# Hybrid decoder layer on Trainium2: in the MLP's fast products, two of seven right sides go through DRAM whole, two sums of weights come first, and the residual is scaled in wider pieces

## The chip, the cores and the metric

The kernel runs on one core of a Trainium2 chip (the chip has eight). The metric is device time in microseconds of one execution of the whole layer. It is compared as a median over several executions; a profiled execution gives the views that are read here. A core has five engines with a queue each: PE (TensorE, matrix products), DVE (VectorE), ACT (ScalarE), POOL (GpSimd) and SP (SyncE, which here issues every DMA). Each engine takes its instructions in the order in which they were put into its queue; one that waits holds up all behind it.

## The reference

One decoder layer over 1024 tokens of width 1024, in float32: two mixers side by side, cross-attention into 256 memory tokens, and a squared-ReLU MLP with a hidden width of 4096. The change lies in the MLP:

```python
D_MODEL = 1024
SEQ = 1024
D_FF = 4 * D_MODEL
...
def rmsnorm(x, g):
    xf = x.astype(jnp.float32)
    y = xf * lax.rsqrt(jnp.mean(xf * xf, axis=-1, keepdims=True) + EPS)
    return (y * g.astype(jnp.float32)).astype(x.dtype)
...
        u = jax.nn.relu(rmsnorm(x, ln2[l]) @ w_ff1[l])
        x = x + (u * u) @ w_ff2[l]
    return rmsnorm(x, ln_f)
```

## The kernel before

Activations lie with features in the partitions (128) and tokens in the free dimension, so a projection takes weights as the stationary side ("left") and activations as the moving side ("right"). A float32 operand is *split* in two parts, a high part `hi` (an ACT copy into the type that PE multiplies) and a low part `lo` = operand minus `hi` (a DVE subtraction): that is `split` (L129 to L136). A product of two split operands is three matmuls into one PSUM bank, lo·hi, hi·lo and hi·hi: `mm3` (L182 to L186).

**Seven products for eight.** Both MLP projections use the Winograd form of Strassen's scheme on 2 by 2 blocks: seven block products in place of eight, of which four take sums of left blocks and four sums of right blocks. The products are numbered 1 to 7; 1, 2 and 4 take plain blocks of the left side, 5, 6, 7 and 3 take sums. The right sides are called "11", "21", "22" and t1 to t4.

**Up projection** (L1169 to L1457). The 4096 hidden rows are cut into 16 *pairs* `p_` of two 128-row tiles, two pairs to each of 8 blocks `b`. `left_up` (L1185) loads two weight tiles r1 = (x11, x12) and r2 = (x21, x22), each 128x1024 (the pair's rooms are `wr` for an odd pair, `z` for an even one), and makes left sides in three groups: group 0 splits r1 as it is (products 1 and 2) and x22 alone into `h22`, `l22` (product 4); then four sums are formed in place, on POOL for pairs 2 to 15 and on DVE for pairs 0 and 1; group 1 splits r2, now two sums (products 5 and 6), and group 2 splits r1, now the other two (products 7 and 3). `jobs` (L1211 to L1215) is the order of the products, a job being 12 matmuls; `prepare` (L1225) cuts left sides five jobs ahead. `Pair.run` (L1326) multiplies, and puts the results together on DVE (`add`, L1324) and ACT (L1313, L1314 for the squared ReLU, L1337 for a copy `p1` of product 1).

**Between the projections** the four blocks u11, u12, u21, u22 of a pair and the sums t1 to t4 are written to DRAM (`right[b]`, a slot for each of the seven right sides with places [0] for hi and [1] for lo). `put` (L1360) splits one 128x512 tile with a hi room that `rotate("d", "e")` takes from two rooms `r_d` and two `r_e`, and stores both parts (L1364, L1365). `put_right` (L1367) lists seven steps for a pair, one step before each job. The last of the eight blocks goes to `plain` in the same way.

**The residual.** While the up projection runs, `stretch` (L1420) takes the residual `x2d` back from DRAM in 16 pieces of 128x512, multiplies each by `row` (L1428, DVE) and stores it again. A piece is loaded into an `r_d` or `r_e` room at one job and scaled two jobs later.

**Down projection** (L1459 to L1517). 28 steps `(b, m)`, seven blocks `b` by four output tiles `m`. `left` (L1398) loads one 128x1024 tile of `w_ff2q` into `wr` (two rooms), forms four sums on POOL (L1408), and splits the plain blocks into two `w4` rooms and the sums into `wh`, `wl`. `rights` (L1461) loads two right sides, hi and lo, into one `act` room; there are seven such rooms, two for the residual and four for the right sides in use, so the first pair of right sides of the next block (products 1 and 5: "11" and t1) finds a free room early. A step multiplies 7 x 2 x 3 = 42 matmuls and adds each product into the residual on DVE (L1515).

The rooms named `w4` (five of 128x1024) are shared by u22 with t1, by t2 with t4 and by the plain left sides of the down projection. The instruction order on each engine follows a list scheduler's simulated times, priorities in the order of the program text.

Of the kernel before, what the change touches and what calls it, by code (L numbers as in the profile page):

```python
# [9 lines left out]
F32 = mybir.dt.float32  # L10
F32R = mybir.dt.float32r
AF = mybir.ActivationFunctionType
ALU = mybir.AluOpType
# [6 lines left out]
TH = 512  # L20
D = 1024
KT = D // P
# [22 lines left out]
def hybrid_layer(ctx: ExitStack, tc: tile.TileContext, a: dict, out: bass.AP):  # L45
    nc = tc.nc
    v, s, g = nc.vector, nc.scalar, nc.gpsimd
# [24 lines left out]
    def w4(shape=(P, 1024), dt=F32):  # L72
        t = sb("w4", [P, 1024], 5, dt)[: shape[0]]
        return t.rearrange("p (a b) -> p a b", b=shape[2]) if len(shape) == 3 else t
# [36 lines left out]
    load = nc.sync.dma_start  # L111
# [17 lines left out]
    def split(hi, lo, src, scale=None):  # L129

        if scale is None:
            s.activation(hi, src, AF.Copy)  # L132
            return v.tensor_tensor(out=lo, in0=src, in1=hi.bitcast(F32), op=ALU.subtract)  # L133
        else:
            s.activation(hi, src, AF.Copy, scale=scale)
            return v.scalar_tensor_tensor(out=lo, in0=src, scalar=scale, in1=hi.bitcast(F32), op0=ALU.mult, op1=ALU.subtract)  # L136
# [24 lines left out]
    def rotate(*tags):  # L161

        spare[tags] = spare.get(tags, -1) + 1
        return w2(tags[spare[tags] % len(tags)])
# [23 lines left out]
    def both(pair, f):  # L188
        return f(pair[0]), f(pair[1])
# [63 lines left out]
    row = const("row", [P, T])  # L253
# [12 lines left out]
    at = 0  # L266
# [33 lines left out]
    h = [(act(), act()), (act(), act())]  # L300
# [20 lines left out]
    for k in range(KT):  # L321
        if k == 2:
            load(wg_raw, a["w_gate"])
        if k % 2 == 0:
            c = slice(k % 4 * 256, k % 4 * 256 + 512)
# [719 lines left out]
    n = 0  # L1045
# [119 lines left out]
    def sub(out_, x, y, by=v):  # L1165
        by.tensor_tensor(out=out_, in0=x, in1=y, op=ALU.subtract)
# [18 lines left out]
    def left_up(p_, group):  # L1185

        if group == 0:
            raws[p_] = raw_pair(p_, *todo[p_][2:])
        r1, r2 = raws[p_]
        x11, x12, x21, x22 = r1[:, :TH], r1[:, TH:], r2[:, :TH], r2[:, TH:]  # L1190
        hi, lo = (sb(t, [P, 1024], 3, F32R) for t in ("wh", "wl"))
        split(hi, lo, (r1, r2, r1)[group])
        if group == 0:
            h22, l22 = (w2(t, dt=F32R) for t in ("bc" if p_ else "ay"))
            split(h22, l22, x22)
            cuts[p_, 4] = both((h22, l22), lambda t: t.rearrange("p (k c) -> p k c", k=4))
            by = g if p_ > 1 else v
            sub(x11, x11, x21, by)
            by.tensor_tensor(out=x21, in0=x21, in1=x22, op=ALU.add)
            sub(x22, x22, x11, by)  # L1200
            sub(x12, x12, x22, by)
        for e in range(2):
            cuts[p_, ((1, 2), (5, 6), (7, 3))[group][e]] = both((hi, lo), lambda t: t[:, e * TH : e * TH + TH].rearrange("p (k c) -> p k c", k=4))
        if group == 2:
            del raws[p_]
# [154 lines left out]
    def put(dst, x):  # L1360

        hi = rotate("d", "e").bitcast(F32R)
        split(hi, x.bitcast(F32R), x)
        load(dst[0], hi.bitcast(F32))  # L1364
        load(dst[1], x)  # L1365

    def put_right(b, k, pair):  # L1367

        u11, u12, u21, u22 = (pair.u[c] for c in ("11", "12", "21", "22"))
        t1 = pair.t1  # L1370
        to = lambda c: [right[b][ORDER.index(c), :, p_, k] for p_ in range(2)]
        t = {}

        def one():
            sub(t1, u12, u11)
            put(to("11"), u11)

        def two():
            x = w4()
            t[2], t[4] = x[:, :TH], x[:, TH:]  # L1380
            sub(t[2], u22, t1)
            sub(u12, u22, u12, g)
            put(to("t1"), t1)

        def four():
            sub(t[4], t[2], u21)
            put(to("22"), u22)

        return [one, two, lambda: put(to("t3"), u12), four, lambda: put(to("21"), u21), lambda: put(to("t2"), t[2]), lambda: put(to("t4"), t[4])]
# [8 lines left out]
    def left(src):  # L1398

        q = sb("wr", [P, 1024], 2)  # L1400
        after[0] = load(q, src)
        q = q.rearrange("p (q c) -> p q c", q=4)
        q21, q11, q12, q22 = (q[:, i] for i in range(4))
        sums = z4()[:, :1024].rearrange("p (q c) -> p q c", q=4)
        s1, s2, s3, s4 = (sums[:, i] for i in range(4))

        for o, x, y, op in ((s1, q21, q22, ALU.add), (s2, s1, q11, ALU.subtract), (s3, q11, q21, ALU.subtract), (s4, s2, q12, ALU.subtract)):
            g.tensor_tensor(out=o, in0=x, in1=y, op=op)  # L1408
        hq, lq = (w4(dt=F32R)[:, :768].rearrange("p (q c) -> p q c", q=3) for _ in range(2))
        split(hq, lq, q[:, 1:])  # L1410
        hs, ls = (sb(t, [P, 1024], 3, F32R).rearrange("p (q c) -> p q c", q=4) for t in ("wh", "wl"))
        split(hs, ls, sums)
        f = lambda hi, lo, i: both((hi, lo), lambda t: t[:, i].rearrange("p (k c) -> p k c", k=2))
        return {1: f(hq, lq, 0), 2: f(hq, lq, 1), 3: f(hs, ls, 3), 4: f(hq, lq, 2), 5: f(hs, ls, 0), 6: f(hs, ls, 1), 7: f(hs, ls, 2)}

    stretches = [(n, hf) for n in range(KT) for hf in range(2)]

    held = []

    def stretch(n, hf):  # L1420

        x = x2d[:, n // 2, n % 2, hf]
        if not held:
            held.append(rotate("d", "e"))
            load(held[0], x)
        else:
            t = held.pop()
            v.tensor_tensor(out=t, in0=t, in1=row[:, hf * TH : hf * TH + TH], op=ALU.mult)  # L1428
            load(x, t)

    pairs = {}
# [1 line left out]
    for at, (p_, i) in enumerate(jobs):  # L1433
        prepare(at)
        for _ in range(2 if at < 2 else 1):
            if rest and at:
                rest.pop(0)()
        if at == 6:
            norm_factors(1)
        if at == 30:  # L1440
            to_row(row, inv, 8, rowd[3:4], bank)
        if at > 30 and at % 2 == 0 and stretches:
            stretch(*stretches[0])
            if at % 4 == 2:
                stretches.pop(0)
        if at == len(jobs) - 3:
            lefts = left(a["w_ff2q"][0, 0])
        if later:
            later.pop(0)()
        pair = pairs.setdefault(p_, Pair(p_))  # L1450
        pair.run(i, cuts.pop((p_, i)))
        if i == 4:
            b, k = todo[p_][:2]
            later += put_right(b, k, pair) if b < NB - 1 else put_plain(k, pair)
            del pairs[p_]
# [5 lines left out]
    def rights(b, at):  # L1461

        t = act()
        n = min(2, 7 - at)
        for e in range(n):
            load(t[:, 4 * e : 4 * e + 4].bitcast(F32), right[b][at + e].rearrange("p e k c -> p (e k) c"))
        return {SEVEN[at + e]: (t[:, 4 * e : 4 * e + 2], t[:, 4 * e + 2 : 4 * e + 4]) for e in range(n)}

    x2 = []

# [3 lines left out]
        load(x2[m // 2][:, m % 2], x2d[:, m])  # L1474

    steps = [(b, m) for b in range(NB - 1) for m in range(4)]
    r = {}
    r.update(rights(0, 0))
    r.update(rights(0, 2))
    x2_load(0)  # L1480
    r.update(rights(0, 4))
# [2 lines left out]
    def distances(op, m):  # L1484

        x = x2[m // 2][:, m % 2]
        for i, hf in ((0, 1), (1, 0)):
            g.tensor_tensor(out=x[:, i, hf], in0=x[:, i, hf], in1=x[:, 1, 1], op=op)

    for at, (b, m) in enumerate(steps):  # L1490
        now = lefts
        if m == 0:
            r_now, r = r, {}
        if at + 1 < len(steps):
            b1, m1 = steps[at + 1]
            lefts = left(a["w_ff2q"][b1, m1])
        with tc.issue_after(after[0].ins):
            if at < 3:
                x2_load(at + 1)
            if b + 1 < NB - 1:  # L1500
                for i in ((), (), (0,), (2, 4, 6))[m]:
                    r.update(rights(b + 1, i))
        if b == 0:
            distances(ALU.subtract, m)
        x = x2[m // 2][:, m % 2]
        x11, x12, x21, x22 = (x[:, i, j] for i in range(2) for j in range(2))
        held = {}

        for i, of, y, op in ((1, 1, x22, ALU.add), (5, 5, x22, ALU.add), (7, 7, x22, ALU.add), (6, 6, x22, ALU.add), (2, 1, x11, ALU.add), (4, 5, x21, ALU.subtract), (3, 7, x12, ALU.subtract)):
            if of == i:  # L1510
                held[of] = bank()
            ps = held[of]
            for k in range(2):
                mm3(ps, both(now[i], lambda t: t[:, k]), both(r_now[i], lambda t: t[:, k]), of == i and k == 0, k == 1, True)
            v.tensor_tensor(out=y, in0=y, in1=ps, op=op)  # L1515
        if b == NB - 2:
            distances(ALU.add, m)  # L1517


    us = []  # L1520
# [107 lines left out]
```

## Time and profile before

| what | value |
|---|---|
| median of three executions (lowest, highest) | 1550.0 us (1548.9, 1554.5) |
| profiled execution | 1552.39 us |
| its span, first to last instruction | 1550.6 us |
| mean granted TensorE clock | 0.995 |
| busy share PE, DVE, ACT, POOL | 97%, 71%, 47%, 29% |
| moved by DMA | 311.94 MB, mean 201 GB/s |

The page of the profile is read by part: busy times by engine, the span in 40 slices, the DMA queues, the chain of work that ended last, the costliest groups of instructions. Beside it stand views of the trace: the timeline of one engine (start, duration, engine, line, operation, output and inputs; in square brackets how long the engine was idle just before, and what ended that), a table of windows (busy time and count by engine in a stretch of time), instruction groups (count, busy time, mean duration) and the waits. Names of tiles stand without their buffer numbers.

### The profile page before, as it was taken

To read this page: it belongs to the slowest core of one execution; us is meant where nothing else is said; L and a number is where in the kernel's file an instruction comes from. 1 tells how busy PE (TensorE), PEld (TensorE's weight loads), DVE (VectorE), ACT (ScalarE), POOL (GpSimd) and SP (SyncE) were. 2 spreads that over 40 slices of the span, in tenths; PEclk is the share of its full clock that TensorE was granted. 3 is DMA by queue.
4 is the path that set the end of the run, shared out by engine and by line. 5 is a ranking of instruction groups with operands and counts; after the bars stand their busy time and mean duration, and the time that the engine had idled before them with its cause. 6 is when DMAs were issued, how large, how long until landed. Compare 5 with 4: busy or idle time off the path is not lost.

```text
span 1550.6 us, 22020 instructions
## 1 busy us (share of the span) xinstructions
PE 1511.7 (97%) x7729; PEld 1260.3 (81%) x7729; DVE 1104.4 (71%) x1742; ACT 722.3 (47%) x1351; POOL 445.1 (29%) x501
## 2 busy tenths in 40 slices
PE   8999999999999999999999999899999999999997
PEld 8878888889898887788888788677778778888887
DVE  7756676665788874844457988788877767766666
ACT  7324343334688773634444556566665422111224
POOL 0002130413455441511110023333333543333320
PEclk9999999999999999999999999999999999999999
DMA  6422323446887949953344458778777976666623
GB/s 216 126 78 82 95 104 114 130 129 164 254 257 220 314 150 304 326 166 118 116 156 146 153 168 283 253 262 288 274 249 277 382 278 243 239 243 240 244 93 110
DMA packets 124412, 311.94 MB, mean 201 GB/s; under 512 B 13822, under 2 KB 28472, under 8 KB 116364
## 3 DMA queue, kind: packets, MB, share of 16 engines
q1 hardware_dynamic: 124300, 310.52, 58.7%
q8 instruction: 61, 1.00, 0.3%
q14 instruction: 51, 0.42, 0.1%
HBM read 206.42 MB, written 104.05 MB: 200 GB/s over the span
## 4 chain that ended last, share of the span: by engine, by line
PE 76%; DVE 9%; DMA 7%; ACT 4%; issue 3%; SPq 0%; POOL 0%; DVEq 0%; POOLq 0%; ACTq 0%
PE tp L184 7%; PE tp L186 7%; PE tp L185 7%; PE mm L184 5%; PE m L184 5%; PE m L186 5%; PE mm L186 5%; PE mm L185 5%; PE m L185 5%; PE sc L184 4%; PE sc L186 4%; PE sc L185 4%; PE ov L779 2%; PE tp L760 2%; PE ov L184 2%
## 5 line engine op out<-in xcount | busy, mean ns | idle before, releaser
L184 PE MATMUL tp<-act,wl 128*128 128x512 f32 (+1 forms) x448 | 176.1, 393 | 3.4 <-DVE wl L133 2.7
L185 PE MATMUL tp<-act,wh 128*128 128x512 f32 (+1 forms) x448 | 175.4, 392 | 0.0
L186 PE MATMUL tp<-act,wh 128*128 128x512 f32 (+1 forms) x448 | 174.9, 392 | 0.0
L132 ACT ACTIVATE wh<-wr 128x1024 fp32r<-128x1024 f32 (+2 forms) x99 | 99.0, 1000 | 90.0 <-PE tp L186 33.2
L133 DVE TENSOR_TENSOR wl<-wr,wh 128x1024 fp32r<-128x1024 f32 (+2 forms) x99 | 120.4, 1216 | 26.5 <-ACT wh L132 26.2
L184 PE MATMUL mm<-act,wl 128*128 128x512 f32 (+1 forms) x336 | 130.4, 388 | 2.4 <-DVE r_e L1071 1.4
L186 PE MATMUL mm<-act,wh 128*128 128x512 f32 (+1 forms) x336 | 129.0, 384 | 0.0
L185 PE MATMUL mm<-act,wh 128*128 128x512 f32 (+1 forms) x336 | 128.7, 383 | 0.0
L184 PE MATMUL m<-act,wl 128*128 128x512 f32 (+1 forms) x312 | 120.4, 386 | 0.9 <-DVE r_a L916 0.9
L186 PE MATMUL m<-act,wh 128*128 128x512 f32 (+1 forms) x312 | 119.3, 382 | 0.0
L185 PE MATMUL m<-act,wh 128*128 128x512 f32 (+1 forms) x312 | 119.1, 382 | 0.0
L184 PE MATMUL sc<-act,wl 128*128 128x512 f32 (+1 forms) x252 | 99.5, 395 | 9.5 <-DVE wl L133 4.9
L184 PEld LDWEIGHTS tp<-act,wl 128*128 128x128 f32 x448 | 84.1, 188 | 24.2 <-DVE wl L133 4.0
L186 PEld LDWEIGHTS tp<-act,wh 128*128 128x128 f32 x448 | 84.2, 188 | 19.3
L185 PEld LDWEIGHTS tp<-act,wh 128*128 128x128 f32 x448 | 84.1, 188 | 18.8
L185 PE MATMUL sc<-act,wh 128*128 128x512 f32 (+1 forms) x252 | 98.6, 391 | 0.0
L132 ACT ACTIVATE w<-wr 128x768 fp32r<-128x768 f32 (+2 forms) x31 | 25.5, 825 | 156.6 <-PE tp L186 86.4
L186 PE MATMUL sc<-act,wh 128*128 128x512 f32 (+1 forms) x252 | 98.4, 391 | 0.0
L1408 POOL TENSOR_TENSOR z<-wr 128x256 f32<-128x256 f32 x56 | 49.7, 908 | 165.3 <-DMA wr<-w_ff2q 137.7
L132 ACT ACTIVATE wh<-z 128x1024 fp32r<-128x1024 f32 (+1 forms) x54 | 55.5, 1027 | 60.2 <-PE sc L186 25.3
L184 PEld LDWEIGHTS mm<-act,wl 128*128 128x128 f32 x336 | 63.3, 188 | 15.7 <-DVE r_e L1071 1.8
L186 PEld LDWEIGHTS mm<-act,wh 128*128 128x128 f32 x336 | 63.1, 188 | 12.8
(671 smaller groups left out, 4220.8 us busy)
## 6 DMA issues: line engine op xcount, KB each, us to landing
act<-right SPq DMA_DIRECT2D x49, 1024.0 KB
right<-w SPq DMA_DIRECT2D x56, 256.0 KB
wr<-w_ff2q SPq DMA_DIRECT2D x28, 512.0 KB
right<-r_d SPq DMA_DIRECT2D x49, 256.0 KB
right<-r_e SPq DMA_DIRECT2D x49, 256.0 KB
act<-fqk SPq DMA_DIRECT2D x48, 256.0 KB
wr<-w_in SPq DMA_DIRECT2D x20, 512.0 KB
wr<-w_ff SPq DMA_DIRECT2D x20, 512.0 KB
```

What stands on the lines that cost most here:

```text
L132: s.activation(hi, src, AF.Copy)
L133: return v.tensor_tensor(out=lo, in0=src, in1=hi.bitcast(F32), op=ALU.subtract)
L184: nc.tensor.matmul(ps, w[1], x[0], start=first, stop=False, skip_group_check=more)
L185: nc.tensor.matmul(ps, w[0], x[1], start=False, stop=False, skip_group_check=more)
L186: nc.tensor.matmul(ps, w[0], x[0], start=False, stop=last, skip_group_check=more)
L760: nc.tensor.transpose(self.ps[:, d * P : (d + 1) * P], self.pts[d][:, self.j * P : (self.j + 1) * P], ident)
L779: nc.tensor.matmul(self.ov[:, c0:], self.fv[:, self.j], t[:, c0:], start=self.j == 0 and t is self.p[1], stop=self.last and t is self.p[0])
L1408: g.tensor_tensor(out=o, in0=x, in1=y, op=op)
```

## The change

In `left_up` the two sums for products 5 and 6 are formed first, from x11, x21 and x22; then come x12 and x11, the latter from the split parts of x22 (`h22`, `l22`), so that five instructions stand where there were four. In `put_right` the right sides "11" and t1 are stored whole, once, in place of a split and two stores. `rights` loads these two (half the bytes) into the lo half of their room, and `split_whole` splits them there: for block 0 after the first loads, for the others at the end of the step that issued the load. `stretch` works on 128x1024 in a `w4` room, 8 pieces, loaded at one job and scaled four jobs later. The left side of the down projection's second step is asked for before the first right sides.

```diff
--- before.py
+++ after.py
@@ -1194,11 +1194,13 @@
             h22, l22 = (w2(t, dt=F32R) for t in ("bc" if p_ else "ay"))
             split(h22, l22, x22)
             cuts[p_, 4] = both((h22, l22), lambda t: t.rearrange("p (k c) -> p k c", k=4))
+
             by = g if p_ > 1 else v
-            sub(x11, x11, x21, by)
             by.tensor_tensor(out=x21, in0=x21, in1=x22, op=ALU.add)
-            sub(x22, x22, x11, by)
+            sub(x22, x21, x11, by)
             sub(x12, x12, x22, by)
+            sub(x11, h22.bitcast(F32), x22, by)
+            by.tensor_tensor(out=x11, in0=x11, in1=l22.bitcast(F32), op=ALU.add)
         for e in range(2):
             cuts[p_, ((1, 2), (5, 6), (7, 3))[group][e]] = both((hi, lo), lambda t: t[:, e * TH : e * TH + TH].rearrange("p (k c) -> p k c", k=4))
         if group == 2:
@@ -1373,14 +1375,14 @@
 
         def one():
             sub(t1, u12, u11)
-            put(to("11"), u11)
+            load(to("11")[1], u11)
 
         def two():
             x = w4()
             t[2], t[4] = x[:, :TH], x[:, TH:]
             sub(t[2], u22, t1)
             sub(u12, u22, u12, g)
-            put(to("t1"), t1)
+            load(to("t1")[1], t1)
 
         def four():
             sub(t[4], t[2], u21)
@@ -1413,19 +1415,19 @@
         f = lambda hi, lo, i: both((hi, lo), lambda t: t[:, i].rearrange("p (k c) -> p k c", k=2))
         return {1: f(hq, lq, 0), 2: f(hq, lq, 1), 3: f(hs, ls, 3), 4: f(hq, lq, 2), 5: f(hs, ls, 0), 6: f(hs, ls, 1), 7: f(hs, ls, 2)}
 
-    stretches = [(n, hf) for n in range(KT) for hf in range(2)]
+    stretches = list(range(KT))
 
     held = []
 
-    def stretch(n, hf):
-
-        x = x2d[:, n // 2, n % 2, hf]
+    def stretch(n):
+
+        x = x2d[:, n // 2, n % 2].rearrange("p h c -> p (h c)")
         if not held:
-            held.append(rotate("d", "e"))
+            held.append(w4())
             load(held[0], x)
         else:
             t = held.pop()
-            v.tensor_tensor(out=t, in0=t, in1=row[:, hf * TH : hf * TH + TH], op=ALU.mult)
+            v.tensor_tensor(out=t, in0=t, in1=row, op=ALU.mult)
             load(x, t)
 
     pairs = {}
@@ -1439,9 +1441,9 @@
             norm_factors(1)
         if at == 30:
             to_row(row, inv, 8, rowd[3:4], bank)
-        if at > 30 and at % 2 == 0 and stretches:
-            stretch(*stretches[0])
-            if at % 4 == 2:
+        if at > 30 and at % 4 == 0 and stretches:
+            stretch(stretches[0])
+            if at % 8 == 4:
                 stretches.pop(0)
         if at == len(jobs) - 3:
             lefts = left(a["w_ff2q"][0, 0])
@@ -1463,8 +1465,19 @@
         t = act()
         n = min(2, 7 - at)
         for e in range(n):
-            load(t[:, 4 * e : 4 * e + 4].bitcast(F32), right[b][at + e].rearrange("p e k c -> p (e k) c"))
+            if at:
+                load(t[:, 4 * e : 4 * e + 4].bitcast(F32), right[b][at + e].rearrange("p e k c -> p (e k) c"))
+            else:
+                load(t[:, 4 * e + 2 : 4 * e + 4].bitcast(F32), right[b][e][:, 1])
+                whole.append((t[:, 4 * e : 4 * e + 2], t[:, 4 * e + 2 : 4 * e + 4]))
         return {SEVEN[at + e]: (t[:, 4 * e : 4 * e + 2], t[:, 4 * e + 2 : 4 * e + 4]) for e in range(n)}
+
+    whole = []
+
+    def split_whole():
+        while whole:
+            hi, lo = whole.pop(0)
+            split(hi, lo, lo.bitcast(F32))
 
     x2 = []
 
@@ -1474,8 +1487,10 @@
         load(x2[m // 2][:, m % 2], x2d[:, m])
 
     steps = [(b, m) for b in range(NB - 1) for m in range(4)]
+    second = left(a["w_ff2q"][steps[1]])
     r = {}
     r.update(rights(0, 0))
+    split_whole()
     r.update(rights(0, 2))
     x2_load(0)
     r.update(rights(0, 4))
@@ -1493,7 +1508,7 @@
             r_now, r = r, {}
         if at + 1 < len(steps):
             b1, m1 = steps[at + 1]
-            lefts = left(a["w_ff2q"][b1, m1])
+            lefts = left(a["w_ff2q"][b1, m1]) if at else second
         with tc.issue_after(after[0].ins):
             if at < 3:
                 x2_load(at + 1)
@@ -1515,6 +1530,7 @@
             v.tensor_tensor(out=y, in0=y, in1=ps, op=op)
         if b == NB - 2:
             distances(ALU.add, m)
+        split_whole()
 
 
     us = []
```

## The prediction

> **What bounds the kernel now.** I read the busy times first, then the windows of the MLP, then PE's timeline for every idle time in it, then the timelines of the other engines just ahead of these.
>
> ```profile
> PE 1511.7 (97%) x7729; PEld 1260.3 (81%) x7729; DVE 1104.4 (71%) x1742; ACT 722.3 (47%) x1351; POOL 445.1 (29%) x501
> ```
> ```profile
> core 0: us, PE busy (x) PEld busy (x) DVE busy (x) ACT busy (x) POOL busy (x), PEclk, DMA share, GB/s
> 884.00:1216.00 332.00, 320.28 (x1361) 254.69 (x1360) 270.57 (x326) 204.21 (x320) 119.74 (x82) 0.99 0.74 259
> 1216.00:1253.00 37.00, 37.00 (x159) 29.39 (x158) 29.90 (x41) 11.36 (x15) 19.22 (x20) 1.00 1.01 385
> 1253.00:1262.00 9.00, 7.08 (x24) 5.33 (x23) 5.31 (x7) 0.85 (x1) 2.10 (x4) 0.81 1.02 419
> 1262.00:1494.00 232.00, 232.00 (x996) 185.92 (x995) 160.60 (x212) 44.36 (x47) 84.39 (x94) 1.00 0.59 226
> ```
>
> PE bounds it. The last row is PE at its pace: 232 us for 996 matmuls, 0.233 us each, no gap. So a job of 12 matmuls takes 2.8 us and a step of 42 takes 9.8 us. The change removes no matmul; all it can win is time in which PE stands still or runs slowly in the MLP. These are all of PE's waits from 884 us to 1494 us that the timeline marks, but for one of 0.7 us at 889:
>
> ```profile
> 977.03 0.50 PE L184 MATMUL sc<-act,wl 128*128 128x512 f32 x1 [0.75 <-DVE wl L133]
> 987.26 0.80 PE L184 MATMUL sc<-act,wl 128*128 128x512 f32 x1 [4.37 <-ACT r_p L1337]
> 988.28 0.63 PE L186 MATMUL sc<-act,wh 128*128 128x512 f32 x1
> 988.71 0.63 PE L184 MATMUL sc<-act,wl 128*128 128x512 f32 x1
> ...
> 1028.74 0.50 PE L184 MATMUL tp<-act,wl 128*128 128x512 f32 x1 [0.75 <-DVE wl L133]
> 1063.11 0.50 PE L184 MATMUL ov<-act,wl 128*128 128x512 f32 x1 [0.20 <-DVE wl L133]
> 1069.58 0.50 PE L184 MATMUL ov<-act,wl 128*128 128x512 f32 x1 [0.48 <-ACT r_p L1337]
> 1111.21 0.50 PE L184 MATMUL sc<-act,wl 128*128 128x512 f32 x1 [2.17 <-DVE wl L133]
> 1111.55 0.40 PE L185 MATMUL sc<-act,wh 128*128 128x512 f32 x1
> 1147.35 0.50 PE L184 MATMUL sc<-act,wl 128*128 128x512 f32 x1 [1.95 <-DVE wl L133]
> 1153.42 0.50 PE L184 MATMUL sc<-act,wl 128*128 128x512 f32 x1 [0.21 <-ACT r_p L1337]
> 1255.29 0.50 PE L184 MATMUL tp<-act,wl 128*128 128x512 f32 x1 [1.92 <-DVE wl L133]
> ```
>
> Eight gaps in the up projection sum to 10.9 us. Each restart costs 0.1 more (1111.21 to 1111.55 is 0.34, not 0.233), 0.8 in all. After the long one the matmuls start 0.43 us apart instead of 0.233 (988.28 to 988.71), for some six: 1.2. Together 12.9. In the down projection there is one gap, 1.92; in the window that holds it 24 matmuls took 7.08 us where 24 x 0.233 is 5.6, so about 1.5 went to the clock (0.81): 3.5 with the gap. **At most 16.4 us can be won.**
>
> **Where these gaps come from.** Two chains make them. The first is the four sums on POOL, here ahead of 1111.21:
>
> ```profile
> 1101.18 0.68 DVE L133 TENSOR_TENSOR r_c<-wr,r_b 128x512 fp32r<-128x512 f32 x1
> 1101.78 1.22 DVE L133 TENSOR_TENSOR wl<-wr,wh 128x1024 fp32r<-128x1024 f32 x1
> ...
> 1104.96 1.67 DVE L133 TENSOR_TENSOR w<-w,r_e 128x512 fp32r<-128x512 f32 x1
> ...
> 1109.95 1.21 DVE L133 TENSOR_TENSOR wl<-wr,wh 128x1024 fp32r<-128x1024 f32 x1
> ```
> ```profile
> 1103.08 1.30 POOL L1166 TENSOR_TENSOR wr<-wr,wr 128x512 f32<-128x512 f32 x1 [7.80 <-DVE wl L133]
> 1104.45 1.62 POOL L1199 TENSOR_TENSOR wr<-wr 128x512 f32<-128x512 f32 x1
> 1106.15 3.32 POOL L1166 TENSOR_TENSOR wr<-wr,wr 128x512 f32<-128x512 f32 x2
> ```
> ```profile
> 1107.81 1.06 ACT L132 ACTIVATE wh<-wr 128x1024 fp32r<-128x1024 f32 x1 [2.22 <-POOL wr L1166]
> ```
>
> POOL's first sum overwrites x11, so it waits for the split of r1 (1101.78, ends 1103.0). The split of r2 needs the third sum, so ACT copies its high part only at 1107.81, DVE the low part at 1109.95, and PE starts at 1111.21. DVE's own work is stretched meanwhile (1.67 for what takes 0.68 alone). The second chain is a hi room that a store has not yet given back:
>
> ```profile
> 973.09 0.63 ACT L132 ACTIVATE r_d<-w 128x512 fp32r<-128x512 f32 x1 [5.01 <-DMA x2d<-r_d]
> ```
> ```profile
> 1142.22 0.63 ACT L132 ACTIVATE r_d<-w 128x512 fp32r<-128x512 f32 x1 [4.55 <-DMA right<-w]
> ```
>
> ACT stands for 5.0 and 4.6 us, and the split of the next left side is queued behind: PE's gaps of 0.75 at 977.03 and of 1.95 at 1147.35.
>
> **The change part by part.**
>
> ```profile
> L133 DVE TENSOR_TENSOR w<-w,r_e 128x512 fp32r<-128x512 f32 x29 | 25.8, 901 | 0.2
> ...
> L133 DVE TENSOR_TENSOR wl<-z,wh 128x1024 fp32r<-128x1024 f32 x23 | 29.1, 1267 | 8.1 <-ACT wh L132 8.1
> ...
> L1428 DVE TENSOR_TENSOR r_d<-r_d,row 128x512 f32<-128x512 f32 x8 | 8.6, 1081 | 6.5 <-DMA r_d<-x2d 6.5
> ```
> ```profile
> L1166 POOL TENSOR_TENSOR z<-z,z 128x512 f32<-128x512 f32 x21 | 32.1, 1529 | 136.4 <-DVE wl L133 127.7 <-DVE r_c L133 7.9
> ```
>
> *Whole right sides.* 14 pairs x 2 = 28 splits and 28 stores of 256 KB leave the up projection: on DVE 28 x 0.90 = 25 us, on ACT 28 x 0.63 (973.09 above) = 18 us, on SP's queue 28 issues. None of this stands in a gap by itself; its worth is the rooms. Before, each pair took 7 hi rooms for puts and about 1.75 for the residual out of four, one every 2.2 us, so a room came round after 9 us; now 5, so every 3.9 us and round after 15.7 us, against a hold of some 6 us (ACT copy, DVE subtraction, a store of 4 to 5 us as the waits show). The two gaps of the second chain should close: **2.7**.
>
> The splits return in the down projection as 14 of 128x1024: 14 x 1.27 = 18 us on DVE, about as much as 14 copies of 1.06, 15 us, on ACT. There DVE is busy 160.6 of 232 us and ACT 44.4, so this lies under PE: 0, and if the cover is gone, the rival on late splits below. Seven loads of 2 MB become 1 MB; two of these (blocks 0 and 1), with the last 1 MB of removed stores, lie at 1180 to 1260 us, where DMA is full (1.01). That is 3 MB or 8 us of DMA at 385 GB/s, just ahead of the gap at 1255, which ends on weights that came late:
>
> ```profile
> 1244.92 1.43 POOL L1408 TENSOR_TENSOR z<-wr 128x256 f32<-128x256 f32 x2 [6.10 <-DMA wr<-w_ff2q]
> ```
>
> The bounds are 0 and 3.5; I take the middle, **1.8**, since the new splits come into the same engines there.
>
> *Two sums first.* x21 + x22 waits for the loads alone, and x22 new only for the split of x22 (1101.18, ends 1101.9), not for r1's. So POOL's path to the split of r2 loses r1's split (1.2), one sum (1.6), and often the first sum too: 3 to 4 us earlier. That is more than the 2.17 at 1111 and the 0.75 at 1028, which has the same shape: **2.9**. The long gap at 987 ends on ACT's copy of product 1, queued behind a square that waited for a DVE slowed by the same four sums; between 0 and 5.6 (clock included) I take two thirds, **3.7**, since the burst is cut in 2 and 3 and less DVE work meets it. Of the three small gaps (0.89) I take half, **0.45**, and of the restarts **0.6**.
>
> The price is a fifth instruction. On POOL 14 x 1.53 = 21 us, which POOL has (119.7 of 332 busy). DVE pays by being stretched: against 0.68, its two-input rows in the up projection carry some 43 us of stretch (the first row above has 29 x 0.22 = 6.4 of it) for 70 POOL operations, 0.6 each, so 14 x 0.6 = 8.6, against 25 + 7 saved. On DVE, for pairs 0 and 1, 2 x 0.69; this falls where DVE has no slack:
>
> ```profile
> 880.00:890.00 10.00, 9.27 (x41) 7.15 (x40) 10.00 (x17) 6.77 (x12) 0.00 (x0) 1.00 0.11 33
> ```
>
> Between 0 and 1.4 I take **-0.7**.
>
> *Wider residual.* The eight pieces in `r_d` rooms took 8.6 us of DVE and, taking the eight in `r_e` rooms for the same, all 17.2; 8 x 1.27 = 10.2 come in their place, and the waits for loads (6.5 in the row) should go, as the scaling now comes four jobs (11.2 us) after the load. Same bytes, 16 issues fewer on SP. Nothing beyond the rooms already counted. *Second left side asked for earlier:* its weights still need a `wr` room of the last pair; 0, between -0.5 and 0.5.
>
> **Sum:** 2.7 + 1.8 + 2.9 + 3.7 + 0.45 + 0.6 - 0.7 = 11.4. The profiled execution took 1552.4 (span 1550.6 and 1.8 around it), so 1541.0; it stood 2.4 above the median, so on the median's basis 1538.6.
>
> **The rivals.** *POOL holds DVE.* Five sums in place of four keep DVE stretched where it is 81% busy (270.6 of 332), and the gaps behind POOL stay: 987, 1028, 1111, the small ones and the restarts. For it: 1104.96 above, 1.67 for 0.68. Against: DVE loses 32 us of other work. Only the rooms and half of 1255 are won, 4.5 - 0.7: 1546. The Trainium skill, SBUF — State Buffer, "Who interferes with whom", says that a DVE instruction with two SBUF inputs and a GpSimd one that reads SBUF exclude each other for the whole of the first to start. By that a new sum can hold DVE for its full length and not for the 0.6 us that I take. The row agrees: the stretched instruction ends about when a POOL one does. With 14 x 1.53 = 21 us of stretch in place of 8.6 the saving on DVE would still be 10 us, so by this rule too the sum keeps its sign.
>
> *Late splits of the whole sides* (slower). DVE and ACT keep their order, and a split of a right side whose load has not landed holds DVE's adds, then PE's banks; or it is done too late for products 1 and 5, the first of a block. A late left side at 1255 cost 3.5 us. At all six block changes after the first that is 21 us: 1538.6 + 21 = 1560. It decides from the point at which the low part ends after the last product of the block before. Against it: two loads of the next but one block go out at 1252.59, a whole block (39 us) ahead, and DVE idles 31% of this time.
>
> ```profile
> 1252.59 1.09 SPq L1466 DMA_DIRECT2D act<-right  x2
> ```
>
> *`w4` rooms in place of hi rooms* (slower). Five rooms serve u22 with t1 (held some 10 jobs and a store of 1.6 jobs, every 7 jobs), t2 with t4 (5 and 1.6, every 7), and now the residual (4 and 1.6, every 8): 1.7 + 0.9 + 0.7 = 3.3 rooms on average. If DVE or SP waits for a store of 4.6 us at each of eight pieces, half of it reaching PE, 18 us: 1557. *The order does not come out as written:* if the scheduler leaves the sums behind other POOL work, only rooms are won: 1547.
>
> **How the numbers follow.** Gaps mostly closed 0.58, at 1538.6, its own range 1534 (all 16.4 won) to 1543. POOL holds DVE 0.18. Order lost 0.05. Late splits 0.13, `w4` rooms 0.06. What a measurement of this kernel can tell from no change is about 0.5%, 7.75 us: faster is below 1542.2. The forecast case lies there but for 0.03, so faster 0.55; same 0.03 + 0.18 + 0.05 = 0.26; slower 0.19. The range 1533 to 1555 leaves out the two slower cases, 0.19.
>
> **What would show it.** Right: no ACT wait on a store of a hi room over 1 us; POOL's first two sums ahead of r1's low part, ACT's `wh` for r2 without a wait on POOL; PE idle in the up projection below 4 us; DVE near 75% there. Wrong: a PE gap at each block change of the down projection, behind a `split` of an `act` room; DVE adds waiting for a store of `w`; PE gaps behind DVE subtractions of 1.6 us and more; DVE full and PE idle near 885 us.

## The result, and the profile after

| | before | after |
|---|---|---|
| median (lowest, highest) of 20 runs each | 1551.94 us (1548.90, 1555.96) | 1550.16 us (1545.51, 1553.21) |
| ratio, 95% interval | | 0.998 [0.9972, 0.9989] |
| span of the profiled execution | 1550.6 us | 1547.3 us |

The change wins about 2 us (3.3 us between the two profiled spans) where 11.4 were forecast. The time lies in the forecast range, the gain does not come near the forecast. First the busy times of after, then its windows over the stretches that were shown of before (columns: time, then busy time and count of PE, PEld (its weight loads), DVE, ACT and POOL, the granted clock, the DMA share, GB/s):

```profile
PE 1510.3 (98%) x7729; PEld 1261.5 (82%) x7729; DVE 1100.9 (71%) x1722; ACT 718.8 (46%) x1337; POOL 483.4 (31%) x515
```
```profile
884.00:1216.00 332.00, 320.77 (x1365) 255.96 (x1364) 256.76 (x295) 188.79 (x294) 150.47 (x96) 0.99 0.67 233
...
1253.00:1262.00 9.00, 9.00 (x41) 7.23 (x40) 5.64 (x9) 1.91 (x2) 5.57 (x8) 1.00 0.84 338
1262.00:1494.00 232.00, 232.00 (x996) 186.94 (x995) 172.74 (x222) 53.77 (x56) 88.08 (x89) 1.00 0.53 204
```

The down projection did what was hoped: 1253 to 1262 us now has PE busy throughout at full clock (before 7.08 us of 9 at 0.81), and the last row is still without a gap although the splits of the right sides are now made there (DVE 172.7 us busy, before 160.6). The up projection lost 13.8 us of DVE work, 15.4 of ACT work and 0.07 of the DMA share, and PE gained 0.5 us from it: 320.8 of 332, before 320.3. PE's timeline in the up projection (start, duration, instruction; in brackets how long PE was idle just before, and what ended that) says why:

```profile
1000.65 0.50 PE L184 MATMUL tp<-act,wl 128*128 128x512 f32 x1 [3.37 <-DVE r_f L1326]
1021.50 0.50 PE L184 MATMUL mm<-act,wl 128*128 128x512 f32 x1 [0.99 <-DVE wl L133]
1063.30 0.50 PE L184 MATMUL sc<-act,wl 128*128 128x512 f32 x1 [2.34 <-DVE r_f L1326]
1126.25 0.50 PE L184 MATMUL ov<-act,wl 128*128 128x512 f32 x1 [2.18 <-DVE r_f L1326]
1147.52 0.50 PE L184 MATMUL sc<-act,wl 128*128 128x512 f32 x1 [1.42 <-DVE wl L133]
1210.07 0.50 PE L184 MATMUL tp<-act,r_c 128*128 128x512 f32 x1 [0.19 <-DVE w L1326]
```

The gaps of before are gone but for one near 1147, which now has another cause, and others stand in their place: 10.5 us, before 10.9. The three largest (7.9 us) end on a row of a kind that no gap of before ended on, `r_f` at L1326: the DVE addition that takes a product out of its PSUM bank. PE cannot start the next product in that bank before it. DVE's timeline ahead of the gap at 1063.30, and SP's issue of the load that its first row waits for:

```profile
1056.90 1.23 DVE L1430 TENSOR_TENSOR w<-w,row 128x1024 f32<-128x1024 f32 x1 [2.22 <-DMA w<-x2d]
1058.04 0.68 DVE L1326 TENSOR_TENSOR r_p<-sc,r_p 128x512 f32<-128x512 f32 x1
1058.64 0.69 DVE L133 TENSOR_TENSOR r_c<-wr,r_b 128x512 fp32r<-128x512 f32 x1
1060.09 1.16 DVE L1166 TENSOR_TENSOR w<-w,r_p 128x512 f32<-128x512 f32 x1 [0.76 <-ACT r_p L1316]
1061.35 0.69 DVE L133 TENSOR_TENSOR r_p<-r_p,r_e 128x512 fp32r<-128x512 f32 x1
1061.96 0.69 DVE L133 TENSOR_TENSOR w<-w,r_d 128x512 fp32r<-128x512 f32 x1
1062.56 0.68 DVE L1326 TENSOR_TENSOR r_f<-sc,r_p 128x512 f32<-128x512 f32 x1
```
```profile
1051.46 0.42 SPq L1427 DMA_DIRECT2D w<-x2d  x1
```

The first DVE row is the residual's multiplication. It stands 2.22 us for its load, which was issued at 1051.46 behind a weight load and had landed 5.4 us later. Behind it in DVE's queue are two PSUM additions; the second ends at 1063.24 and PE starts at 1063.30. The wait stands six instructions ahead of the row that ends the gap. Ahead of 1000.65 and 1126.25 stand the same rows in the same order (multiplications at 994.26 and 1119.84, waits of 1.55 and 2.28). The gaps at 1021.50 and 1147.52 end on a low part `wl` that stands third behind a multiplication (1017.49 and 1143.90, waits of 1.87 and 1.59), its `wh` done before. So a waiting multiplication stands close ahead of all five gaps of more than 0.2 us, on DVE. The reverse does not hold: three of the eight waits, the longest of 4.29 us among them, made no gap. There the `r_f` addition starts 3.5 us behind the multiplication, where it takes 5.7 us ahead of the three largest gaps:

```profile
1035.74 1.23 DVE L1430 TENSOR_TENSOR w<-w,row 128x1024 f32<-128x1024 f32 x1 [2.69 <-DMA w<-x2d]
...
1039.22 0.68 DVE L1326 TENSOR_TENSOR r_f<-sc,r_p 128x512 f32<-128x512 f32 x1
```

From DVE's groups between 905 and 1216 us (count, busy, mean ns, idle before):

```profile
L133 DVE TENSOR_TENSOR wl<-z,wh 128x1024 fp32r<-128x1024 f32 x23 | 35.5, 1542 | 7.6 <-ACT wh L132 7.6
...
L1430 DVE TENSOR_TENSOR w<-w,row 128x1024 f32<-128x1024 f32 x8 | 10.2, 1275 | 19.0 <-DMA w<-x2d 19.0
```

All eight pieces waited, 19.0 us in sum. Before, five of the sixteen pieces waited, 6.5 us in the row the prediction shows and 2.2 in that of the `r_e` rooms. The text of the program puts four jobs between load and multiplication; the trace has 4.9 to 7.1 us from issue to start. The first row shows the second suspect: with five sums on POOL a low part of 128x1024 takes 1.54 us on average, before 1.27.

### The profile page after: what moved, and what is told of

It is laid out like the page before. It is cut to its first block, busy times and chain, and to the rows that moved or that the text cites. A ratio compares the mean times of both kernels' runs of the same rounds, so it can differ in the third digit from the quotient of the medians.

```text
span 1547.3 us, 21934 instructions
## 1 busy us (share of the span) xinstructions
PE 1510.3 (98%) x7729; PEld 1261.5 (82%) x7729; DVE 1100.9 (71%) x1722; ACT 718.8 (46%) x1337; POOL 483.4 (31%) x515
## 4 chain that ended last, share of the span: by engine, by line
PE 82%; DMA 7%; DVE 6%; issue 2%; ACT 2%; POOL 0%; SPq 0%; DVEq 0%; POOLq 0%; ACTq 0%
PE tp L184 7%; PE tp L186 7%; PE tp L185 7%; PE mm L184 5%; PE sc L184 5%; PE sc L186 5%; PE sc L185 5%; PE mm L186 5%; PE mm L185 5%; PE m L184 5%; PE m L186 5%; PE m L185 5%; PE ov L184 2%; PE ov L185 2%; PE ov L186 2%
## 5 line engine op out<-in xcount | busy, mean ns | idle before, releaser
L133 DVE TENSOR_TENSOR wl<-wr,wh 128x1024 fp32r<-128x1024 f32 (+2 forms) x99 | 126.3, 1276 | 26.7 <-ACT wh L132 26.3
L1410 POOL TENSOR_TENSOR z<-wr 128x256 f32<-128x256 f32 x56 | 53.5, 976 | 150.4 <-DMA wr<-w_ff2q 127.9
L133 DVE TENSOR_TENSOR wl<-z,wh 128x1024 fp32r<-128x1024 f32 (+1 forms) x54 | 73.1, 1353 | 12.4 <-ACT wh L132 12.3
```

## The experiments

Two theories stood against each other, called W and P in the expectations. **W**: the multiplication waits for its load ahead of PSUM additions. **P**: POOL's five sums stretch DVE's splits, so that these come late (the rival *POOL holds DVE*). The instruction order of each variant is made anew by the scheduler, so an edit also moves instructions that it does not name; ratios are to the kernel before, measured beside it on the same chip, with 95% intervals.

| kernel | median us | ratio |
|---|---|---|
| after, multiplication late | 1538.50 | 0.9909 [0.9897, 0.9922] |
| the same once more, other chip | 1541.72 | 0.9924 [0.9905, 0.9943] |
| after, first half of the multiplications late | 1543.59 | 0.9941 [0.9923, 0.9960] |
| after, four sums as before | 1549.29 | 0.998 [0.9968, 0.9992] |
| after, multiplication late, four sums | 1541.70 | 0.9923 [0.9910, 0.9937] |
| after, residual in halves as before | 1552.34 | 1.000 [0.9991, 1.0009] |
| before, wide residual alone | 1548.88 | 0.998 [0.9970, 0.9990] |
| before, wide residual and multiplication late | 1551.78 | 0.999 [0.9982, 0.9999] |
| before, multiplication late alone | 1560.35 | 1.0054 [1.0041, 1.0068] |
| before, five sums alone | 1557.14 | 1.0022 [1.0012, 1.0031] |
| after, multiplication late, no early second left side | 1541.82 | 0.9926 [0.9909, 0.9944] |
| after, multiplication late, sums in another order | 1534.10 | 0.9878 [0.9859, 0.9898] |

**The multiplication late.** It is put into DVE's queue behind the last PSUM addition that the program has issued by then; the load stays where it was. Taken in order, the pieces are now multiplied 15.7 to 35.4 us behind the issue of their loads, 23.6 on average where after has 5.8, so the edit moves them by more than a few instructions.

```diff
@@ Pair.run, add
-            v.tensor_tensor(out=out_, in0=ps, in1=x, op=ALU.add)
+            last_add[0] = v.tensor_tensor(out=out_, in0=ps, in1=x, op=ALU.add)
@@ stretch
-            v.tensor_tensor(out=t, in0=t, in1=row, op=ALU.mult)
+            with tc.issue_after(last_add[0].ins):
+                v.tensor_tensor(out=t, in0=t, in1=row, op=ALU.mult)
```

> The changed kernel, with the multiplication of a residual piece put behind the last PSUM add that precedes it in the program. Theory W (DVE stands at the multiplication for a load in flight, and PSUM adds queued behind it come late): DVE's wait for x2d falls from 19.0 us to under 3, PE's gaps of 3.37, 2.34 and 2.18 us and the 1.5 us of slow clock go, 8 to 9 us: ratio to before about 0.993. Theory P (the fifth sum on POOL stretches DVE, that makes the gaps): DVE's subtractions stay stretched, wl at 1.5 us, the time stays at the changed kernel's 0.998.

The median is 1538.5 us. DVE's groups, DVE's timeline at the place that made the gap of 2.34 us in after, and all of PE's gaps in the up projection:

```profile
L133 DVE TENSOR_TENSOR wl<-z,wh 128x1024 fp32r<-128x1024 f32 x24 | 39.6, 1650 | 5.3 <-ACT wh L132 5.3
...
L1433 DVE TENSOR_TENSOR w<-w,row 128x1024 f32<-128x1024 f32 x8 | 11.6, 1456 | 0.0
```
```profile
1051.03 0.68 DVE L1328 TENSOR_TENSOR r_p<-sc,r_p 128x512 f32<-128x512 f32 x1
...
1055.55 0.68 DVE L1328 TENSOR_TENSOR r_f<-sc,r_p 128x512 f32<-128x512 f32 x1
1056.15 1.22 DVE L1433 TENSOR_TENSOR w<-w,row 128x1024 f32<-128x1024 f32 x1
```
```profile
1016.18 0.50 PE L184 MATMUL mm<-act,wl 128*128 128x512 f32 x1 [0.84 <-DVE wl L133]
1056.29 0.50 PE L184 MATMUL sc<-act,wl 128*128 128x512 f32 x1 [0.64 <-DVE r_f L1328]
1076.40 0.50 PE L184 MATMUL tp<-act,wl 128*128 128x512 f32 x1 [0.25 <-DVE wl L133]
1116.91 0.50 PE L184 MATMUL ov<-act,wl 128*128 128x512 f32 x1 [1.04 <-DVE r_f L1328]
1180.78 0.50 PE L184 MATMUL mm<-act,wl 128*128 128x512 f32 x1 [2.01 <-DVE wl L133]
```

The multiplication at this place, now that of the fourth piece (load issued at 1025.49), stands behind both additions, finds its data there, and the waits are 0. PE's gaps fall from 10.5 to 4.8 us. The low parts are stretched more than in after (1.65 against 1.54 us), and the kernel is still 0.7% faster than after, a little more than W had put it at (0.993): W holds, and P does not set the time. On another chip the same kernel gave 0.9924:

> The changed kernel with the late multiplication for all pieces, once more beside the others of this call: ratio 0.991.

**Half of them late.** The order is imposed on the first four pieces only (`if n < 4`).

> The changed kernel with the late multiplication for the first four residual pieces only; the last four stand in DVE's queue where the changed kernel has them. Theory W: DVE waits some 9 us for x2d, all of it after 1040 us; PE's gaps before that go, those near 1060 and 1125 us stay; about half of the 11 us between the two: ratio 0.994 to 0.996. If the late version is faster for another reason (another order on all engines), no such split by time.

0.9941 lies between after and the late kernel; its interval overlaps that of the late kernel beside it, so the split shows in the gaps more than in the time. Three waits are left, all with the last three pieces, 5.7 us. DVE's timeline around the fifth and the seventh piece, and PE's gaps behind them:

```profile
1052.37 1.21 DVE L1434 TENSOR_TENSOR w<-w,row 128x1024 f32<-128x1024 f32 x1
1053.50 0.68 DVE L1328 TENSOR_TENSOR r_p<-sc,r_p 128x512 f32<-128x512 f32 x1
...
1113.23 1.23 DVE L1434 TENSOR_TENSOR w<-w,row 128x1024 f32<-128x1024 f32 x1 [1.72 <-DMA w<-x2d]
```
```profile
1058.75 0.50 PE L184 MATMUL sc<-act,wl 128*128 128x512 f32 x1 [1.93 <-DVE r_f L1328]
1119.63 0.50 PE L184 MATMUL ov<-act,wl 128*128 128x512 f32 x1 [1.82 <-DVE r_f L1328]
```

After's gap at 1000 is gone with the wait ahead of it; that at 1126 stays, as 1.82 at 1119.63, with its wait of 1.72. The gap at 1058.75 shows a second half of the mechanism: here the multiplication waits for nothing, but stands ahead of the `r_p` addition and takes 1.13 us until that starts; the gap is 1.93, where the fully late kernel, with the multiplication behind, has 0.64 at the same product, and after, with the multiplication in this place and a wait of 2.22, has 2.34. So the place alone costs about its duration, and at this product the gap with the wait is only 0.4 us longer. How the whole gain divides between place and wait was not measured.

**Four sums as before**, in after. It takes P's cause away and leaves W's.

```diff
             by = g if p_ > 1 else v
+            sub(x11, x11, x21, by)
             by.tensor_tensor(out=x21, in0=x21, in1=x22, op=ALU.add)
-            sub(x22, x21, x11, by)
+            sub(x22, x22, x11, by)
             sub(x12, x12, x22, by)
-            sub(x11, h22.bitcast(F32), x22, by)
-            by.tensor_tensor(out=x11, in0=x11, in1=l22.bitcast(F32), op=ALU.add)
```

> The changed kernel, with the four sums of before in place of the five. Theory W: the wait for loads stays near 19 us and the split of the two sums comes later again, so no faster than the changed kernel: ratio 0.998 to 1.003. Theory P: wl falls from 1.53 to about 1.24 us, the gaps behind DVE go, ratio 0.993 to 0.995.

```profile
L133 DVE TENSOR_TENSOR wl<-z,wh 128x1024 fp32r<-128x1024 f32 x23 | 30.0, 1305 | 7.2 <-ACT wh L132 7.2
...
L1429 DVE TENSOR_TENSOR w<-w,row 128x1024 f32<-128x1024 f32 x8 | 9.8, 1221 | 12.4 <-DMA w<-x2d 12.4
```

DVE's groups show the low part back at 1.31 us, and the time is that of after: P as the only cause falls. The waits fell too, to 12.4 us, where W had them near 19. The gaps (10.9 us between 1003 and 1190) end mostly on `wl` now, as in before: the old chain through the four sums is back. It starts with the multiplication. DVE, then POOL, ahead of the gap of 2.56 us at 1066.69:

```profile
1054.33 1.23 DVE L1429 TENSOR_TENSOR w<-w,row 128x1024 f32<-128x1024 f32 x1 [2.20 <-DMA w<-x2d]
...
1056.67 1.22 DVE L133 TENSOR_TENSOR wl<-wr,wh 128x1024 fp32r<-128x1024 f32 x1
```
```profile
1057.96 1.29 POOL L1166 TENSOR_TENSOR wr<-wr,wr 128x512 f32<-128x512 f32 x1 [7.81 <-DVE wl L133]
```

POOL's first sum starts as the low part of r1 ends, and that stands third behind a waiting multiplication. The same rows stand ahead of the gaps of 2.34 and 2.89 us (waits of 2.13 and 3.48).

**Both: late, and four sums.**

> The changed kernel with the late multiplication, and the four sums of before in place of the five. If two sums first are worth what the prediction said once the wait for loads is gone (2.9 us and a part of 3.7), PE again waits behind the third sum: 3 to 6 us slower than the late version with five sums (0.991), ratio 0.993 to 0.995. If the fifth sum's stretch of DVE eats that, no difference: 0.991.

0.9923, where the late kernel with five sums gave 0.9909 and 0.9924. The medians' ratios differ by 2 us at most and the intervals overlap, so these runs do not tell the worth of the two sums first from 0. This is the worth with the fifth sum paid: whether there is a gain that the fifth sum eats is not shown by this pair.

**Residual in halves as before**, with whole right sides and five sums.

> The changed kernel, with the residual again in 16 pieces of 128x512 in hi rooms, scaled two jobs after the load. Theory W: the wait for loads falls to the 9 us that before had, the three gaps shrink to about half, ratio 0.994 to 0.997. Theory P: no difference to the changed kernel, 0.998.

1.000 [0.9991, 1.0009], which neither theory had expected. The waits for residual loads are only 6.6 us, some ACT waits on stores of hi rooms are back (7.0 us), and PE still has nine gaps that sum to 13.4 us between 981 and 1175. The three largest (2.65, 2.71, 2.55) end on an `r_f` addition, and none has a multiplication ahead that waits for its piece. Ahead of the first one a multiplication stands 3.56 us for the table `row` (970.88); ahead of the other two it stands directly before the `r_p` addition without a wait (1041.05 and 1104.47), and DVE has just stood 1.2 us for POOL's `r_f`. Why this kernel is slower than after stays open.

**Wide residual alone**, put into before.

> The kernel before, with the wide residual pieces alone. Theory W: DVE waits some 19 us for x2d in place of 8.7, with new PE gaps behind PSUM adds: slower than before by 2 to 6 us, ratio 1.001 to 1.004. Theory P: DVE has 7 us less work and hi rooms come free sooner, nothing new on POOL: faster, ratio 0.996 to 0.999.

0.998, though W as I had put it gave this kernel a loss. Only four of the eight pieces wait, 6.9 us in all: a 4 KB room is no fault by itself. It costs when the queue puts the multiplication ahead of additions that PE needs soon, worse where its load has not landed, and that depends on what else is in the queue.

**Parts of the repair in before.** The multiplication late alone; and wide and late together, but without whole right sides and with the four sums.

> The kernel before with the late multiplication alone, residual in 16 pieces in hi rooms. Theory W: the 8.7 us in which DVE waits for loads go, but a hi room is held longer and ACT waits more for rooms than its 27 us of before: ratio 0.996 to 1.000. If the late multiplication were all that matters: 0.991.

> The kernel before with wide residual pieces and the late multiplication: no whole right sides, four sums. If the whole right sides are worth their rooms (2.7 us) and the gap at 1255 us (1.8 us or more): ratio 0.994 to 0.996, with ACT still waiting about 10 us for stores of hi rooms. If they are worth nothing: 0.991.

The first is slower than before, 1.0054, which was not expected. The second, 0.999, was expected at 0.991 to 0.996. It differs from *late, and four sums* only by the whole right sides (with the second left side, worth nothing below), and the two were measured side by side: 1551.78 against 1541.70, so with the late order these are worth 10.1 us. Without it they are worth nothing that can be told: four sums in after and the wide residual alone, which differ by the same, both gave 0.998. ACT's waits in the first kernel (line, waited for, us in total, times, longest), then in the second, with a row of its timeline there and a gap:

```profile
ACT r_e L132 <- DMA right<-r_e: 23.3, 12, 5.1
ACT r_d L132 <- DMA right<-r_d: 17.2, 15, 4.1
...
ACT r_e L132 <- DMA x2d<-r_e: 9.8, 6, 2.6
```
```profile
ACT r_e L132 <- DMA right<-r_e: 5.4, 3, 3.7
```
```profile
1035.59 0.63 ACT L132 ACTIVATE r_e<-w 128x512 fp32r<-128x512 f32 x1 [3.75 <-DMA right<-r_e]
```
```profile
1255.45 0.50 PE L184 MATMUL tp<-act,wl 128*128 128x512 f32 x1 [1.92 <-DVE wl L133]
```

In the first, a piece that is multiplied later keeps its hi room longer (28.2 us on average from the issue of its load to the multiplication, before 4.8), and ACT stands 50.3 us, by these rows, for stores out of the four rooms, where before stands some 27. Late multiplications must not hold hi rooms, which the wide ones do not. In the second the rooms still serve 28 more splits than after, and 1255.45 is before's gap, as long to the hundredth: the DMA traffic that the whole sides save is not saved. Ahead of its gap of 2.85 us at 1048.24 ACT stood 3.75 us for a store of a hi room (1035.59), and the splits behind came late. Its other large gaps (2.90, 1.54 and 1.29) have none of over 0.9 us in the 10 us ahead, so where all of the 10.1 us lie was not traced.

**Five sums alone**, in before.

> The kernel before with the five sums alone. By the prediction's terms (2.9 + 3.7 + 0.45 - 0.7): ratio 0.996. If DVE's stretch and its other waits eat that: 0.999 to 1.003, with wl at 1.5 us in place of 1.24.

1.0022, slower than before. DVE's timeline ahead of a gap of 2.50 us at 957.83, then ahead of one of 4.70 us at 1024.71:

```profile
955.87 0.69 DVE L1429 TENSOR_TENSOR r_e<-r_e,row 128x512 f32<-128x512 f32 x1 [4.94 <-DMA r_e<-x2d]
...
957.09 0.68 DVE L1325 TENSOR_TENSOR r_f<-sc,r_p 128x512 f32<-128x512 f32 x1
```
```profile
1018.18 0.69 DVE L1429 TENSOR_TENSOR r_d<-r_d,row 128x512 f32<-128x512 f32 x1 [1.48 <-DMA r_d<-x2d]
```

It is the shape of after's gaps, with half pieces: the waiting multiplication comes into the queue ahead of the additions here too. So it is not the width of the piece that brings it there. In the gap of 4.70 the wait and the multiplication make up 2.2 us; the rest was not traced.

**No early second left side**, with the multiplication late.

> The late version, with the left side of the second step of the down projection asked for where before had it. By the prediction it is worth nothing: ratio 0.991.

0.9926 against 0.9924 beside it: no worth that can be told from 0.

**The sums in another order**, with the multiplication late. The two weight tiles are loaded as (x11, x21) and (x12, x22). Four sums do again, and x11 and x12 are split in halves of 512 as soon as they are there:

```diff
-            load(raw, a["w_ff1"][n])
+            load(raw.rearrange("p (n c) -> p n c", n=2), a["w_ff1"][n0 : n1 + 1 : n1 - n0, :, i * TH : i * TH + TH].rearrange("n p c -> p n c"))
...
+            split(hi[:, :TH], lo[:, :TH], x11)
...
+            split(hi[:, TH:], lo[:, TH:], x12)
...
             by.tensor_tensor(out=x21, in0=x21, in1=x22, op=ALU.add)
-            sub(x22, x21, x11, by)
-            sub(x12, x12, x22, by)
-            sub(x11, h22.bitcast(F32), x22, by)
-            by.tensor_tensor(out=x11, in0=x11, in1=l22.bitcast(F32), op=ALU.add)
+            sub(x11, x21, x11, by)
+            sub(x12, x12, x11, by)
+            sub(x22, x22, x11, by)
```

> The late version with the weights loaded as (x11, x21) and (x12, x22), and four sums, the two for products 5 and 6 first: S1 in x21, S2 in x11, then S4 in x12 and S3 in x22; x11 and x12 split in two pieces for products 1 and 2. One POOL operation less in each pair, 14 x 1.5 us, so DVE's wl back at about 1.3 us; one more split of 128x512 in each pair (0.2 us more on DVE and on ACT). If DVE's stretch still costs PE's last gaps (4.8 us in all), ratio 0.988 to 0.990; if these come from elsewhere, 0.991.

1534.10 us, 0.9878 [0.9859, 0.9898]: faster than both kernels, and 7.6 us under the late kernel beside it. The window of the up projection, and DVE's group of low parts:

```profile
884.00:1216.00 332.00, 331.37 (x1424) 266.46 (x1423) 268.63 (x324) 199.23 (x317) 138.69 (x89) 1.00 0.72 250
```
```profile
L133 DVE TENSOR_TENSOR wl<-z,wh 128x1024 fp32r<-128x1024 f32 x17 | 27.0, 1586 | 3.5 <-ACT wh L132 3.4
```

PE is busy 331.4 of 332 us; the one gap that is left in both projections is of 0.50, at 889. The low parts are as long as ever (1.59 us, where a fall to 1.3 had been expected); there are fewer of that size (17 here, 23 in after). Whether the missing fifth sum, the shorter way to the second left side or the new queue order closed the last gaps was not separated.

## Why the prediction was wrong

**The step that failed is the wider residual,** a term put at nothing: "the waits for loads (6.5 in the row) should go, as the scaling now comes four jobs (11.2 us) after the load", with "Nothing beyond the rooms already counted". The four jobs stand in the text of the program; the queue had the multiplication start 4.9 to 7.1 us behind the issue of its load, as soon as that had landed. The waits grew from 8.7 to 19.0 us, and five of the eight had PSUM additions or a low part close behind them that came late for PE. I took a distance in the text for one in DVE's queue. Why the scheduler puts it there was not measured; that it counts on an earlier landing of the load is an argument, not shown. The price is shown: with the order imposed, the same kernel takes 1538.5 and 1541.7 us, so the place of the multiplication, with its wait, takes 0.6 to 0.7% (0.9909 and 0.9924 against 0.998). The width itself is not at fault, since wide pieces alone gave 0.998 in before and the return to halves 1.000 in after.

That the repaired kernel lands at the forecast (1538.6 of 1550.0, 0.993) is in part luck: its gain is made up otherwise than the sum was. The sum adds its terms, and two parts pay only together. With wide pieces and four sums throughout, the ratio is 0.998 with neither, 0.999 with the late order alone, 0.998 with the whole right sides alone, and 0.9923 with both.

**Rooms and whole right sides** were right in kind. ACT's waits on DMA in the up projection of after are for loads, bar 0.9 us; the largest:

```profile
ACT r_b L132 <- DMA z<-w_ff: 4.2, 1, 4.2
```

The stores of hi rooms that stood here before (7.8, 6.6 and 5.0 us for the largest) are gone, and the gap at 1255 went wholly: 3.5, not 1.8. The size was too low: 2.7 and 1.8 make 4.5, the comparison of two kernels gives 10.1. But it pays only with the late order.

**Two sums first** was too high: 7.05 with the small gaps, measured at nothing that can be told from 0 with the late multiplication and a loss of 0.2% alone. The mechanism ran in part: PE's gaps at 987, 1028 and 1111 are gone from after, but ACT still waits for POOL ahead of a split of r2, 1.09 us here where before has 2.22 at 1107.81, and its waits for POOL's sums of the up projection's weights add up to 10.5 us, before 7.0:

```profile
1103.39 1.06 ACT L132 ACTIVATE wh<-wr 128x1024 fp32r<-128x1024 f32 x1 [1.09 <-POOL wr L1166]
```

Behind these chains the additions on DVE came last next. I closed each gap by its own releaser and did not ask what DVE's queue held beside it. The row was there in before: ahead of its longest gap, 4.37 us at 987.26, a stretched multiplication of the residual stands directly before a PSUM addition, and the prediction put this gap down to a DVE slowed by the four sums:

```profile
982.23 1.77 DVE L1428 TENSOR_TENSOR r_e<-r_e,row 128x512 f32<-128x512 f32 x1
983.92 0.68 DVE L1324 TENSOR_TENSOR r_f<-sc,r_f 128x512 f32<-128x512 f32 x1
```

**The smaller terms.** The second left side is worth 0 as far as the runs tell, as said. POOL was 30.7 us more busy in the up projection (150.5, before 119.7), where 21 were reckoned. DVE ended at 256.8 of 332 us, 77%, near the 75% that I named.

**The rivals.** *POOL holds DVE* has its stretch, 1.27 to 1.54 us, and not its consequence: taking it away left 0.998, and the fastest kernels have it. By the rule of the Trainium skill, SBUF — State Buffer, "Who interferes with whom", a DVE instruction with two SBUF inputs and a GpSimd one that reads SBUF exclude each other; the longer DVE rows agree in kind, and the time did not follow them. The prediction's own row fits loosely: the DVE instruction at 1104.96 ends at 1106.63, 0.56 us behind the POOL one. *Late splits of the whole sides* did not occur: 232.00 of 232 us of PE in the down projection. *`w4` rooms* did not either: in after's up projection DVE waits for no store, and ACT for one of `w`, 0.7 us (0.2 more for one of `r_p`). *Order lost* was the nearest in kind, but I had looked for it on POOL and gave it the sums; it was the multiplication on DVE.

## What to carry to other kernels

A distance between a load and its user is worth what the user's queue makes of it: look there, in the trace, for the place that the scheduler chose, and where an engine also frees the banks of the bounding one, force work that can wait behind that. A wait on a shared engine shows up several instructions later under another name, so follow a PE gap back along the engine that ended it to the first instruction with idle time in its brackets. Parts of a change that serve one engine are not priced by adding their gaps: here the whole right sides, the wide pieces and the late multiplication are worth 0.8% together, and none of the parts tried alone brought more than 0.2%. Only changing two of them in turn showed which ones need each other.

## What was not expected of the hardware

The granted clock did not follow the length of a gap. In after a gap of 2.34 us cost clock, one of 3.37 did not (windows of 20 us around the gaps at 1000.65 and 1063.30, and the 4 us behind the second):

```profile
1000.00:1020.00 20.00, 19.35 (x83) 15.64 (x84) 14.42 (x18) 13.23 (x21) 9.67 (x6) 1.00 0.69 238
1060.00:1080.00 20.00, 17.66 (x70) 13.79 (x69) 15.68 (x17) 12.44 (x21) 8.73 (x7) 0.91 0.59 204
1063.30:1067.30 4.00, 4.00 (x11) 3.13 (x12) 3.91 (x4) 2.10 (x4) 2.78 (x2) 0.57 0.78 290
```

In 1060 to 1080 PE is idle for 2.34 us but does 70 matmuls, where 20 us at its pace hold 86: the gap is worth 10 of them, and the other six, 1.4 us, went to the clock, which stood at 0.57 in the 4 us behind it. So of these two gaps the longer cost its length and the shorter 60% more than its length; what decides between the two is not shown.
